# A one-layer streaming encoder step: adds that read PSUM become ScalarE copies and GpSimd adds, squares and norms of output rows stand half a block later, and two tiles' last products come before their norms

## The chip, the cores and the metric

One core of one Trainium2 chip runs the whole program. The metric is the device time of one execution in microseconds, median of several runs. The kernel before takes 1325.29 us (three runs, 1322.95 to 1325.57).

## What is computed

One layer with three branches over a prompt of 2048 tokens (batch 1) and a sample group of 64 tokens with a cache of 1024. Everything is float32. Cut to what matters here:

```
h = rms_norm(x, g_norm);  z = h @ w_in            # 1024 -> 3072
q_sb, k_sb, v_sb, g_sb, u_pool, g_pool, q_xa, g_xa = split(z)
# stick-breaking attention, 8 heads of 64, strictly causal:
s = q_sb . k_sb / 8
w = exp(log_sigmoid(s) + sum over later keys of log_sigmoid(-s))
o_sb = w @ v_sb
o_pool = pooling mixer(u_pool);  o_xa = softmax attention over 256 memory tokens
mixed = concat[o_sb * silu(g_sb), o_pool * silu(g_pool), o_xa * silu(g_xa)]
y = rms_norm(x + mixed @ w_out, g_final)          # the final norm, row by row
```

The outputs are y for both groups, the new key and value rows, the pooling history and the memory keys and values.

## The kernel before

Products are made of two or three float32r passes (a high and a low part of each factor), so TensorE has several matmuls per tile of the result. Up to about 690 us the kernel norms x, makes the projections of `w_in`, the pooling branch, the cross-attention and the sample group's attention. The change touches only what follows: the stick-breaking attention of the prompt, with the output product `mixed @ w_out` run beside it, and a tail that holds the last four row tiles' output product.

**The attention stage.** The prompt's queries go in four stages `s` of 512 tokens (0 to 3). A stage goes over four pairs of heads `p`, and for each over key blocks `j` of 512 from the diagonal back to 0. `Block.score` makes the scores of 128 queries by 512 keys for two heads in a PSUM tile `z` (two of them), `weigh` lets ScalarE take the sigmoid into a slot of the ring `c` (L207) and VectorE run the product from the last key to the first as two scans (L212 on the diagonal, L214 elsewhere). A half-block (`Stream.step`) is two such 128-query tiles, so four scans. Three half-blocks later (`TURN`) `turn` transposes the weights on TensorE into PSUM tiles `pt`, ScalarE copies them to `w` (L230), and `gather` multiplies them with differences of values into `av` (L241), one PSUM buffer. At the last key block of a pair, L252 on VectorE adds `vt` to `av`, which frees `av`; GpSimd multiplies with the gate (L258) and stores to `mix_d` (L259). In the trace's names `at_hl`, `at_hh`, `more_c` and `ends` are slots of these rings.

**The output rows.** From the second stage on, `Rows` holds one tile of 128 tokens of the stage before (12 such tiles, and one of 64 for the sample group). `split` makes its high and low parts: a ScalarE cast (L1098), a GpSimd subtraction (L1099). `piece` makes one of 16 products (two halves of 512 columns, eight each) into `acc`, one PSUM buffer (L1119). At the eighth, L1122 on VectorE adds `acc` to the row in `xt`, which frees `acc`, and L1123 squares the half with a sum. After the second half, `finish` makes the inverse root on VectorE (L1131 and L122 to L131), scales both halves (L1135) and has GpSimd's queue store the row (L1139).

**What sets the order.** For TensorE, ScalarE and VectorE the written order is the program's order in this part; GpSimd's and SyncE's instructions are placed by a scheduler. `Stream.step` writes a half-block: transposes, scores, scans, then as many pieces as `credit` allows (a `None` behind each half's last piece ends a run), then the products with values. The code written inside a piece lands on VectorE behind the scans of that half-block.

**The tail.** With `done` set, `z` takes the place of `acc`, so two tiles can be open at once. `most` makes the first seven products of both halves, `rest_of` the last ones, which need the last pair's result, and then the norm, with a square root on ScalarE (`root_of`).

Of the kernel before, what the change touches and what calls it, by code (L numbers as in the profile page):

```python
# [13 lines left out]
ALU = mybir.AluOpType  # L14
# [4 lines left out]
P = 128  # L19
# [5 lines left out]
KT = D // P  # L25
# [18 lines left out]
def tile_hybrid_step(  # L44
# [30 lines left out]
    V, A, G, PE = nc.vector, nc.scalar, nc.gpsimd, nc.tensor  # L75
# [100 lines left out]
    class Block:  # L176


        def __init__(self, a, j):
            self.a, self.j = a, j  # L180
            p, room = a["p"], a["room"]
            self.K = room("K").rearrange("p (a t) -> p a t", a=2)
            dma(f(self.K), k_d[p][:, j])
            self.V = f(room("V")).rearrange("p (b d) -> p b d", b=4)
            dma(self.V, dv_d[p][:, j])
            self.diag = j == a["s"]
            self.later, a["c"] = a["c"], [None] * 4
# [46 lines left out]
        def gather(self, kb, i0, turned):  # L234

            a, j = self.a, self.j
            room, p, s = a["room"], a["p"], a["s"]
            if self.diag and kb == 0:
                a["av"] = room("av")
            for h, rows in enumerate((LO, HI)):  # L240
                PE.matmul(  # L241
                    a["av"][rows, i0 * P :], self.V[:, kb, rows], turned[:, h, i0 * P :],
                    start=(self.diag and kb == 0), stop=(j == 0 and kb == 3),
                )
            if j == 0 and kb == 0:
                cols = slice(512 * s, 512 * s + 512)
                a["vt"], a["sg"] = room("vt"), room("sg")
                dma(a["vt"], vt_d[p][:, cols])
                dma(a["sg"], sg_d[p][:, cols])
            if j == 0 and kb == 3:  # L250
                o = room("o")
                V.tensor_tensor(o, a["av"], a["vt"], ALU.add)  # L252
                if (s, p) == LAST:

                    V.tensor_tensor(o, o, a["sg"], ALU.mult)
                    last_mixed.append(o)
                else:
                    G.tensor_tensor(o, o, a["sg"], ALU.mult)  # L258
                    store(mix_d[s][:, p], o)  # L259

    class Stream:
# [3 lines left out]


        def __init__(self, more):
            self.halves, self.pieces, self.credit = [], [], 0.0
            self.rate, self.more = 0.0, more

        def step(self, block, g):
            t = len(self.halves)
            self.halves.append((block, g))
            self.credit += self.rate
            turned = []
            b, old = self.halves[t - TURN] if t >= TURN else (None, 0)
            if b is not None:
                turned.append(b.turn(2 * old))
            if block is not None:
                first, second = block.score(2 * g), block.score(2 * g + 1)  # L280
                first()
            if b is not None:
                turned.append(b.turn(2 * old + 1))
            if block is not None:
                second()
                if g == 1:
                    block.cs = block.a["c"]
            self.run(self.credit)
            for what in turned:
                b.gather(*what)  # L290
            self.credit = min(self.credit, 6.0)

        def run(self, n):

            n = min(n, self.credit)
            while n >= 1.0 and self.piece():
                n -= 1.0
                self.credit -= 1.0

        def piece(self):  # L300

            if not self.pieces:
                self.pieces += self.more()
            if self.pieces:
                thunk = self.pieces.pop(0)
                if thunk is not None:
                    thunk()
                    return True
            return False
# [154 lines left out]
    def project(w, n, chunk):  # L464
        for piece in projection(w, n, chunk):
            acc = piece()
            slots.tick()
        return acc
# [180 lines left out]
    for c in range(2):  # L649
        for j in range(2):  # L650
            w, rows = WINDOWS[2 * c + j], slice(64 * j, 64 * j + 64)
# [115 lines left out]
    def cross(p, u, qx):  # L767
# [39 lines left out]
        for delay, stage, i in zip(XSLOTS, (scores, scores, turn, gather, turn, gather), (0, 1, 0, 0, 1, 1)):  # L807
            slots.after(delay, lambda stage=stage, i=i: stage(i))
# [214 lines left out]
    def room(name):  # L1023
        if name == "pt":
            return ps_t.tile([P, 512], F32, tag="pt", name="pt")
        rings[name].append(rings[name].pop(0))
        return rings[name][-1]


    wo = {}  # L1030

    def wo_part(c, part):
        return wo[(c // 4, part)][:, D * (c % 4) : D * (c % 4) + D]
# [14 lines left out]
    class Rows:  # L1048
# [56 lines left out]
        def piece(self, half, c):  # L1105
            n, xt = self.n, self.xt
            cols = slice(512 * half, 512 * half + 512)
            if c == 0 and done and half == 0:
                self.z = room("z")
            if c == 0 and not done:  # L1110
                self.acc = room("acc")
            k = self.ks[c]
            out, mh, ml = self.z[:, half] if done else self.acc, self.mh[:, k], self.ml[:, k]
            wh, wl = wo_part(k, "h")[:, cols], wo_part(k, "l")[:, cols]
            passes = [(out, mh, wh), (out, ml, wh)][: 2 if n == P else 1] + [(out[:n], mh[:, :n], wl)]
            if c == 7:
                passes.reverse()
            for i, (o, m, w) in enumerate(passes):
                PE.matmul(o, m, w, start=(c == i == 0), stop=(c == 7 and i == len(passes) - 1))  # L1119
            if c == 7:  # L1120
                for i in range(0, P, n):
                    V.tensor_tensor(xt[:n, cols], out[i : i + n], xt[:n, cols], ALU.add)  # L1122
                V.scalar_tensor_tensor(  # L1123
                    wo["sq"][:n, cols], xt[:n, cols], 1.0, xt[:n, cols], ALU.mult, ALU.mult,
                    accum_out=self.total[:n, half : half + 1],
                )

        def finish(self):
            n, xt = self.n, self.xt
# [14 lines left out]
    def follow():  # L1144
        if ready and not following:
            following.append(Rows(ready.pop(0)))

    def output_rows():

        if len(settled) >= SETTLED:  # L1150
            follow()
        if not following:
            return []

        if not done and len(stream.halves) - following[0].born < 2:
            return []
        rows = following.pop()
        while rows.parts:
            rows.split()
        pieces = []  # L1160
        for half in range(2):
            for c in range(KT):

                def piece(half=half, c=c):
                    rows.piece(half, c)
                    i = KT * half + c
                    if i == 1:
                        follow()
                    elif i > 3 and (i - 1) % 3 == 0 and following:
                        following[0].split()  # L1170
                    if i == 15:
                        rows.finish()

                pieces.append(piece)
                if c == KT - 1 and not done:
                    pieces.append(None)
        return pieces

    ready, done = [], False
# [17 lines left out]
    stream, tail = Stream(more), []  # L1197
# [19 lines left out]
    def prepared(t, *parts):  # L1217
        rows = Rows(t, parts)
        while rows.parts:
            rows.split()  # L1220
        tail.append(rows)
# [5 lines left out]
            tail[0].split()  # L1227
    while stream.pieces or ready or following:
        stream.piece()
    tail[0].split_late()  # L1230
    tail.append(Rows(T // P - 3, ("K", "K")))


    done = True

    def most(rows):
        for half in range(2):
            for c in range(KT - 1):
                rows.piece(half, c)

    def rest_of(rows):
        for half in range(2):
            rows.piece(half, KT - 1)
        rows.finish()

    for half in range(2):
        for c in range(KT - 1):
# [4 lines left out]
    prepared(T // P - 2, "K", "K")  # L1252
    tail[2].split_late()
    most(tail[1])
    rest_of(tail[0])
    rest_of(tail[1])
    prepared(T // P - 1, "q", "q")
    tail[3].split_late()
    for rows in tail[2:]:
        most(rows)  # L1260
        rest_of(rows)
# [32 lines left out]
```

## Time and profile before

| what | value |
|---|---|
| median of the runs | 1325.29 us |
| the profiled execution | 1323.47 us, of which 1321.7 us span from the first to the last instruction |
| mean granted TensorE clock | 0.981 |
| busy in the span | TensorE 1236.6 us (94%), VectorE 799.7 (61%), ScalarE 520.5 (39%), GpSimd 338.6 (26%) |
| VectorE's scans, L214 (192) and L212 (128) | 252.6 us and 103.8 us, all in the attention |

The span divides into the stages of the attention by the first sigmoid of each: stage 0 from 687 us, stage 1 from 753 us, stage 2 from 857 us, stage 3 from 1039 us, the tail from 1261 us. Busy shares over the whole span say little here, since VectorE is nearly unused in some stretches and nearly full in others: the stage in which an instruction stands has to be looked at by itself. A wait of TensorE is shown with the instruction that ended it, which can be queued behind others on its own engine.

### The profile page before, as it was taken

The page shows a single profiled execution, that of the slowest core. Times are in us where ns is not written, and L with a number is a line of the kernel's source. Part 1 is how long each engine was busy: PE and PEld are TensorE (multiplying, and loading weights), DVE is VectorE, ACT ScalarE, POOL GpSimd, SP SyncE. Part 2 cuts the span into 40 slices and gives each one's busy share as a digit, 9 for nine tenths or more (in the row PEclk, how much of TensorE's full clock was granted, in tenths as well). Part 3 has the DMA queues.
Part 4 walks back from the last instruction along what each step waited for, and adds up shares of the span by engine and source line. Part 5 has one row for each costly group of instructions (what it writes and reads, how often), then busy time and mean ns, then how long its engine had stood idle before and what let it go on. Part 6 is the DMA issues. An engine that isn't in the chain of part 4 may idle for free.

```text
span 1321.7 us, 22014 instructions
## 1 busy us (share of the span) xinstructions
PE 1236.6 (94%) x8506; PEld 954.7 (72%) x8506; DVE 799.7 (61%) x1388; ACT 520.5 (39%) x1077; POOL 338.6 (26%) x415
## 2 busy tenths in 40 slices
PE   5899999999999999999999988999988998999987
PEld 5788888688888888887887755666655655666565
DVE  7863445455554442333224596779987787899644
ACT  5641111144444442231013464446445465576510
POOL 3211237234444442222001113321312002012110
PEclk9999999999999999999999999989999998999999
DMA  7534432555555543443256774434443243431221
GB/s 243 189 121 151 150 132 82 172 177 194 172 167 160 171 143 125 146 131 107 87 182 212 286 269 135 154 104 147 134 136 116 101 127 120 136 112 51 93 74 49
DMA packets 115637, 190.30 MB, mean 144 GB/s; under 512 B 9458, under 2 KB 73548, under 8 KB 115532
## 3 DMA queue, kind: packets, MB, share of 16 engines
q1 hardware_dynamic: 95436, 120.95, 29.9%
q0 software_dynamic: 20096, 67.94, 14.2%
q8 instruction: 67, 1.10, 0.4%
q14 instruction: 38, 0.31, 0.1%
HBM read 118.83 MB, written 70.02 MB: 143 GB/s over the span
## 4 chain that ended last, share of the span: by engine, by line
PE 59%; DVE 10%; issue 7%; ACT 4%; POOL 3%; DMA 3%; DVEq 0%; ACTq 0%; SPq 0%; POOLq 0%
PE acc L1119 11%; PE acc L441 8%; PE acc L443 7%; PE acc L442 7%; PE av L241 7%; DVE at_hl L214 5%; PE pt L227 5%; PE z L198 4%; PE z L1119 3%; ACT more_w L230 2%; ACT at_hl L207 1%; POOL psum_w L669 1%; PE pt_p L787 1%; PE pt_r L477 1%; DVE xo L1122 1%
## 5 line engine op out<-in xcount | busy, mean ns | idle before, releaser
L441 PE MATMUL acc<-hh,wh 128*128 128x512 f32 (+2 forms) x960 | 358.3, 374 | 6.5 <-DVE sg L543 5.5
L442 PE MATMUL acc<-hl,wh 128*128 128x512 f32 (+2 forms) x960 | 341.9, 356 | 0.0
L443 PE MATMUL acc<-hh,wl 128*128 128x512 f32 (+2 forms) x960 | 339.9, 355 | 0.0
L230 ACT COPY more_w<-pt 128x512 f32<-128x512 f32 (+3 forms) x320 | 152.0, 528 | 216.6 <-PE pt L227 214.7
L214 DVE TENSOR_TENSOR_SCAN at_hl<-at_hl,at_hl 128x512 f32<-128x512 f32 x148 | 195.1, 1375 | 25.3 <-ACT at_hl L207 25.3
L441 PEld LDWEIGHTS acc<-hh,wh 128*128 128x128 f32 x960 | 182.0, 190 | 32.4 <-DVE sg L543 8.1
L443 PEld LDWEIGHTS acc<-hh,wl 128*128 128x128 f32 x960 | 181.7, 189 | 24.5 <-issue 1.0
L442 PEld LDWEIGHTS acc<-hl,wh 128*128 128x128 f32 x960 | 182.5, 190 | 21.1 <-issue 4.0
L241 PE MATMUL av<-more_w,at_hh 128*64 128x512 f32 (+3 forms) x640 | 140.0, 551 | 11.3 <-DVE ends L252 8.6
L227 PEld LDWEIGHTS pt<-edge,at_hl 64*128 64x128 f32 x1936 | 87.9, 139 | 60.6 <-issue 44.8
L207 ACT ACTIVATE at_hl<-z 128x1024 f32<-128x1024 f32 (+3 forms) x143 | 130.8, 916 | 0.6
L212 DVE TENSOR_TENSOR_SCAN at_hl<-at_hl,edge 128x128 f32<-128x128 f32 (+3 forms) x116 | 92.8, 852 | 34.4 <-ACT at_hl L207 34.4
L1119 PE MATMUL acc<-at_hh,mh 128*128 128x512 f32 x208 | 92.0, 442 | 19.2 <-DVE xo L1122 14.4
L227 PE MATMUL pt<-edge,at_hl 64*128 64x64 f32 x1936 | 102.3, 228 | 5.5 <-ACT more_w L230 3.7
L1099 POOL TENSOR_TENSOR ml<-m,mh 128x256 fp32r<-128x256 f32 (+1 forms) x52 | 58.9, 1144 | 169.2 <-ACT mh L1098 169.0
L241 PEld LDWEIGHTS av<-more_w,at_hh 128*64 128x64 f32 x640 | 37.9, 137 | 79.3 <-issue 48.1
L1119 PE MATMUL acc<-at_hl,mh 128*128 128x512 f32 (+1 forms) x208 | 84.3, 418 | 0.0
L1119 PE MATMUL acc<-at_hh,ml 128*128 128x512 f32 x192 | 79.5, 414 | 1.0 <-POOL ml L1099 1.0
L198 PE MATMUL z<-at_hh 64*128 64x512 f32 (+2 forms) x576 | 70.2, 375 | 0.0
L432 DVE CAST wh<-wr 128x1024 fp32r<-128x1024 f32 x32 | 23.6, 736 | 70.5 <-PE acc L442 34.2
L1119 PEld LDWEIGHTS acc<-at_hh,mh 128*128 128x128 f32 x208 | 41.8, 201 | 32.5 <-DVE xo L1122 15.7
L543 DVE TENSOR_TENSOR sg<-acc,sg 128x512 f32<-128x512 f32 x24 | 16.5, 690 | 69.9 <-ACT sg L542 69.9
(275 smaller groups left out, 1808.0 us busy)
## 6 DMA issues: line engine op xcount, KB each, us to landing
at_hh<-k_d SPq DMA_DIRECT2D x40, 512.0 KB, 5.3
wr<-in_w_in_dram SPq DMA_DIRECT2D x24, 512.0 KB, 4.7
at_hh<-dv_d SPq DMA_DIRECT2D x40, 256.0 KB, 3.5
xt_x<-in_x_prompt_dram SPq DMA_DIRECT2D x16, 512.0 KB, 4.0
xq<-qx_d SPq DMA_DIRECT2D x64, 128.0 KB, 4.0
k_d<-k POOLq DMA_DIRECT2D x16, 512.0 KB, 3.8
out_dram<-rt POOLq DMA_DIRECT2D x32, 256.0 KB, 3.5
q_d<-q POOLq DMA_DIRECT2D x16, 512.0 KB, 2.9
```

Source lines behind the costliest of these rows:

```text
L198: PE.matmul(z[:, h, :w], a["q"][rows, part, at], K[rows, keys, :w], start=(part == keys == 0), stop=(part == 1),)
L207: A.activation(c[:, :, :n], z[:, :, :n], AF.Sigmoid, scale=-1.0)
L212: V.tensor_tensor_scan(cc, cc, edge[:, 512 - n :][:, ::-1], 0.0, ALU.mult, ALU.max)
L214: V.tensor_tensor_scan(cc, cc, cc, self.later[i][:, h, 0:1], ALU.mult, ALU.bypass)
L227: PE.transpose(pt[:, h, i], c, ident[rows, rows])
L230: A.copy(w[:, :, i0:, rows], pt[:, :, i0:])
L241: PE.matmul(a["av"][rows, i0 * P :], self.V[:, kb, rows], turned[:, h, i0 * P :], start=(self.diag and kb == 0), stop=(j == 0 and kb == 3),)
L441: PE.matmul(out, wh[:, k], hi, start=(k == 0), stop=False)
L442: PE.matmul(out, wh[:, k], lo, start=False, stop=False)
L443: PE.matmul(out, wl[:, k], hi, start=False, stop=(k == KT - 1))
L1099: engine.tensor_tensor(ml, m, f(mh), ALU.subtract)
L1119: PE.matmul(o, m, w, start=(c == i == 0), stop=(c == 7 and i == len(passes) - 1))
```

## The change

Four edits:

- In `gather`, L252's add on VectorE becomes a ScalarE copy of `av` into `o` and a GpSimd add of `vt` (15 of 16; the last pair of the last stage keeps the old form).
- In `Rows.piece`, for the 12 tiles of 128 rows beside the attention (24 halves), L1122's add becomes a ScalarE copy of `acc` into `wo["sq"]` and a GpSimd add into `xt`. The sample tile and the tail keep the old form.
- For those 24 halves the square, and for all 13 tiles the norm (`finish`), go to a list `due`, which is written out by `settle` in the next half-block, behind that half-block's scans.
- In the tail, `rest_of` takes the first two tiles together: both tiles' last products, adds and squares are written before both norms.

```diff
@@ gather
             if j == 0 and kb == 3:
                 o = room("o")
-                V.tensor_tensor(o, a["av"], a["vt"], ALU.add)
                 if (s, p) == LAST:
 
+                    V.tensor_tensor(o, a["av"], a["vt"], ALU.add)
                     V.tensor_tensor(o, o, a["sg"], ALU.mult)
                     last_mixed.append(o)
                 else:
+                    A.copy(o, a["av"])
+                    G.tensor_tensor(o, o, a["vt"], ALU.add)
                     G.tensor_tensor(o, o, a["sg"], ALU.mult)
                     store(mix_d[s][:, p], o)
@@ Stream.step
                 second()
                 if g == 1:
                     block.cs = block.a["c"]
+            self.settle()
             self.run(self.credit)
...
+        def settle(self):
+
+            while self.due:
+                self.due.pop(0)()
@@ Rows.piece
             if c == 7:
-                for i in range(0, P, n):
-                    V.tensor_tensor(xt[:n, cols], out[i : i + n], xt[:n, cols], ALU.add)
-                V.scalar_tensor_tensor(
-                    wo["sq"][:n, cols], xt[:n, cols], 1.0, xt[:n, cols], ALU.mult, ALU.mult,
-                    accum_out=self.total[:n, half : half + 1],
-                )
+                if n == P and not done:
+
+                    A.copy(wo["sq"][:, cols], out)
+                    G.tensor_tensor(xt[:, cols], wo["sq"][:, cols], xt[:, cols], ALU.add)
+                    stream.due.append(lambda: self.square(half))
+                else:
+                    for i in range(0, P, n):
+                        V.tensor_tensor(xt[:n, cols], out[i : i + n], xt[:n, cols], ALU.add)
+                    self.square(half)
+
+        def square(self, half):
+            n, cols = self.n, slice(512 * half, 512 * half + 512)
+            V.scalar_tensor_tensor(
+                wo["sq"][:n, cols], self.xt[:n, cols], 1.0, self.xt[:n, cols], ALU.mult, ALU.mult,
+                accum_out=self.total[:n, half : half + 1],
+            )
@@ output_rows
                     if i == 15:
-                        rows.finish()
+                        stream.due.append(rows.finish)
@@ the tail
-    def rest_of(rows):
-        for half in range(2):
-            rows.piece(half, KT - 1)
-        rows.finish()
+    def rest_of(*tiles):
+        for rows in tiles:
+            for half in range(2):
+                rows.piece(half, KT - 1)
+        for rows in tiles:
+            rows.finish()
...
-    rest_of(tail[0])
-    rest_of(tail[1])
+    rest_of(*tail[:2])
```

The order of TensorE's instructions is the same in both programs. Three places on the other engines show the move. In the changed file the lines are L258 to L260 (copy, add and product of the attention result), L1131 and L1132 (copy and add of a row half), L1136 (the add that stays), L1141 (square), L1149 and L1153 (norm). The order view names the scans SCALAR_TENSOR_TENSOR.

VectorE, end of the second row tile (stage 1), before: the last steps of its norm, then the attention add, the four scans of the next half-block, and the add and square of the third tile's first half.

```order
L130 TENSOR_TENSOR nr_t<-nr_t,nr_y 128x1
L131 SCALAR_TENSOR_TENSOR nr_y<-nr_t,nr_y 128x1
L1135 SCALAR_TENSOR_TENSOR xo<-xo,nr_y,gf 128x512 x2
L252 TENSOR_TENSOR at_hl_6504<-av,ends 128x512
L214 SCALAR_TENSOR_TENSOR at_hl_6504<-at_hl_6504,at_hl_6506 128x512 x4
L1122 TENSOR_TENSOR xo<-acc_6518,xo 128x512
L1123 SCALAR_TENSOR_TENSOR sq,total_o<-xo 128x512
```

The norm stood ahead of the half-block's scans, and the two adds that free `av` and `acc` stood between and behind scans. VectorE, the same tile, now:

```order
L212 SCALAR_TENSOR_TENSOR at_hl_6506<-at_hl_6506,edge 128x512 x2
L1141 SCALAR_TENSOR_TENSOR sq,total_o<-xo 128x512
L214 SCALAR_TENSOR_TENSOR more_c_6512<-more_c_6512,at_hl_6506 128x512 x2
L214 SCALAR_TENSOR_TENSOR at_hl_6504<-at_hl_6504,at_hl_6506 128x512 x6
L1141 SCALAR_TENSOR_TENSOR sq,total_o<-xo 128x512
L1149 TENSOR_TENSOR total_s<-total_o 128x1
```

No add is left among the scans; the second square and the norm follow the scans of one more half-block. ScalarE, same place, now, where the two copies (L1131 of `acc`, L258 of `av`) stand between one half-block's second sigmoid and the next one's copies of transposes:

```order
L207 ACTIVATE more_c_6512<-z_6515 128x1024
L230 COPY more_w<-pt 128x8x64 x2
L207 ACTIVATE at_hl_6504<-z_6516 128x1024
L1131 COPY sq<-acc_6518 128x512
L258 COPY at_hl_6504<-av 128x512
L230 COPY more_w<-pt 128x8x64 x2
```

Before, nothing stood there. VectorE in the tail, now, from the first tile's second half to the first norm:

```order
L1136 TENSOR_TENSOR xo<-z_6515,xo 128x512
L1141 SCALAR_TENSOR_TENSOR sq,total_o<-xo 128x512
L1136 TENSOR_TENSOR at_hl_6506<-z_6516,at_hl_6506 128x512
L1141 SCALAR_TENSOR_TENSOR sq,total_o<-at_hl_6506 128x512
L1149 TENSOR_TENSOR total_s<-total_o 128x1
L139 TENSOR_SCALAR nr_v<-total_s 128x1
```

Before, the first tile's whole norm stood ahead of the second tile's first add.

## Rows read from the trace of the kernel before

**Rows 1.** Waits of TensorE, 753 to 1321 us: total us, times, longest.

```profile
PE acc L1119 <- DVE xo L1122: 14.4, 9, 3.5
PE av L241 <- DVE ends L252: 8.6, 3, 4.1
```

**Rows 2.** The same by stretch: 857 to 1039, 753 to 793, 1039 to 1245.

```profile
PE acc L1119 <- DVE xo L1122: 11.0, 5, 3.5
PE av L241 <- DVE ends L252: 4.1, 1, 4.1
...
PE av L241 <- DVE ends L252: 2.7, 1, 2.7
PE av L241 <- DVE at_hl L252: 0.9, 1, 0.9
...
PE acc L1119 <- DVE xo L1122: 2.9, 3, 1.8
```

**Rows 3.** Busy us by stretch: PE, PEld, DVE, ACT, POOL, then clock, DMA, GB/s.

```profile
753.00:793.00 40.00, 35.12 (x392) 22.02 (x392) 36.38 (x39) 28.06 (x56) 7.34 (x6) 0.96 0.83 291
793.00:857.00 64.00, 58.38 (x448) 40.41 (x446) 45.26 (x72) 28.54 (x56) 20.00 (x18) 0.97 0.44 143
857.00:1039.00 182.00, 166.17 (x1397) 110.10 (x1393) 151.02 (x215) 90.42 (x168) 42.70 (x38) 0.95 0.41 126
1039.00:1245.00 206.00, 196.25 (x1793) 124.53 (x1792) 177.23 (x234) 122.47 (x211) 29.60 (x29) 0.98 0.36 110
```

**Rows 4.** Timeline of VectorE and TensorE around 857 us: start, us, what.

```profile
854.01 6.62 DVE L214 TENSOR_TENSOR_SCAN at_hl<-at_hl,at_hl 128x512 f32<-128x512 f32 x4
860.56 0.66 DVE L1122 TENSOR_TENSOR xo<-acc,xo 128x512 f32<-128x512 f32 x1
...
861.27 0.80 PE L1119 MATMUL acc<-at_hh,mh 128*128 128x512 f32 x1 [3.47 <-DVE xo L1122]
```

**Rows 5.** Busy us in stretches of half clock (columns as in Rows 3).

```profile
860.70:867.40 6.70, 6.13 (x14) 4.79 (x15) 3.03 (x7) 0.00 (x0) 0.45 (x1) 0.50 0.13 51
925.60:928.90 3.30, 3.30 (x10) 2.11 (x9) 3.30 (x3) 0.00 (x0) 2.25 (x2) 0.50 0.36 97
973.30:976.70 3.40, 3.40 (x16) 1.00 (x18) 3.40 (x3) 0.00 (x0) 2.65 (x3) 0.50 0.65 239
1024.50:1027.90 3.40, 3.25 (x8) 2.57 (x9) 3.37 (x6) 0.00 (x0) 0.04 (x1) 0.50 0.07 29
1065.50:1068.80 3.30, 3.30 (x10) 2.17 (x10) 3.30 (x5) 0.00 (x0) 0.00 (x0) 0.50 0.45 133
...
1287.40:1290.70 3.30, 3.30 (x8) 2.62 (x9) 2.19 (x7) 0.01 (x1) 0.00 (x0) 0.50 0.27 103
```

**Rows 6.** Groups by shape, 753 to 1250: count | busy us, mean ns | idle before.

```profile
L214 DVE TENSOR_TENSOR_SCAN at_hl<-at_hl,at_hl 128x512 f32<-128x512 f32 x148 | 195.1, 1375 | 25.3 <-ACT at_hl L207 25.3
...
L1122 DVE TENSOR_TENSOR xo<-acc,xo 128x512 f32<-128x512 f32 x23 | 15.4, 667 | 18.3 <-PE acc L1119 18.3
...
L252 DVE TENSOR_TENSOR at_hl<-av,ends 128x512 f32<-128x512 f32 x7 | 4.7, 675 | 0.3 <-issue 0.3
...
L230 ACT COPY more_w<-pt 128x512 f32<-128x512 f32 x214 | 115.1, 590 | 169.2 <-PE pt L227 168.3
```

**Rows 7.** Timeline: VectorE's scans and GpSimd's products, 757 to 771 us.

```profile
767.46 1.27 DVE L214 TENSOR_TENSOR_SCAN at_hl<-at_hl,at_hl 128x512 f32<-128x512 f32 x1
768.65 2.22 DVE L214 TENSOR_TENSOR_SCAN at_hl<-at_hl,at_hl 128x512 f32<-128x512 f32 x1
...
757.09 1.27 POOL L258 TENSOR_TENSOR at_hl<-at_hl,ends 128x512 f32<-128x512 f32 x1 [4.11 <-DVE at_hl L252]
...
767.63 2.16 POOL L258 TENSOR_TENSOR ends<-ends 128x512 f32<-128x512 f32 x1 [8.39 <-DVE ends L252]
```

**Rows 8.** Timeline of VectorE and TensorE in the tail.

```profile
1283.97 0.16 DVE L1131 TENSOR_TENSOR total_s<-total_o 128x1 f32<-128x1 f32 x1
...
1286.60 0.68 DVE L1122 TENSOR_TENSOR at_hl<-z,at_hl 128x512 f32<-128x512 f32 x1
...
1287.34 0.80 PE L1119 MATMUL z<-at_hl,at_hh 128*128 128x512 f32 x1 [4.18 <-DVE at_hl L1122]
```

More of the change, by code (lines that the diff above doesn't have):

```diff
@@ L267, in __init__ @@
         def __init__(self, more):
-            self.halves, self.pieces, self.credit = [], [], 0.0
+            self.halves, self.pieces, self.credit, self.due = [], [], 0.0, []
             self.rate, self.more = 0.0, more
@@ L1229, in tile_hybrid_step @@
         stream.piece()
+    stream.settle()
     tail[0].split_late()
```

## The prediction

> **What bounds the kernel now.** I read the waits of TensorE first, because TensorE is busy almost throughout the part that the change touches. From 753 us on it loses 14.4 us in nine waits for L1122, the add that frees `acc`, and 8.6 us in three for L252, the add that frees `av` [rows 1]; a fourth wait for L252, of 0.9 us, stands in the early stretch [rows 2]. That is 23.9 us. The timeline shows what such a wait is. At 857.8 us TensorE wants `acc`. The add takes only 0.66 us, but it stands behind four scans that began at 854.01 and took 6.62 us [rows 4]. So the wait is VectorE's queue, not the add.
>
> Next I read the granted clock behind these waits. After five of them TensorE runs at half clock, 1.2 instead of 2.4 GHz, for 6.7, 3.3, 3.4, 3.4 and 3.3 us [rows 5]. TensorE is at work nearly all of those 20.1 us, so the level costs half of them, about 10.0 us.
>
> Last, the busy time by stretch. From 753 to 793 us VectorE is busy 36.38 of 40 us, 91%: there it is the bound, and a wait of TensorE only says where TensorE meets it. From 857 to 1039 us it has 151.02 of 182 us, from 1039 to 1245 us 177.23 of 206, from 793 to 857 us 45.26 of 64 [rows 3].
>
> **The copies on ScalarE.** 39 copies of 128x512 from PSUM are added; copies of this shape take 0.590 us in the mean [rows 6]. Each stands behind the half-block's second sigmoid and ahead of copies for which ScalarE waits on TensorE anyway (168.3 us of such waits [rows 6]). I cost them at nothing. If that cover were gone they would cost 39 x 0.59 = 23 us. What they bring is that `acc` and `av` come free about 0.8 us after their last product, while TensorE has other products and transposes to do. I take both kinds of wait as gone, with the low clock behind them, except where VectorE binds.
>
> **The adds on GpSimd and VectorE's load.** VectorE sheds an add of 0.667 us (row halves) or 0.675 us (attention) [rows 6], 39 in all: 14 from 857 to 1039 us, 12 from 1039 to 1245, 6 from 793 to 857, 3 from 753 to 793, the others at the two ends. GpSimd takes an add of the size of its product L258: 1.27 us when no scan runs beside it, 2.16 us beside scans. The scan beside the latter takes 2.22 us, where the one before it took 1.27 [rows 7]: 0.95 us lost on VectorE. No row shows what an added add will cost VectorE. It lies between 0 (GpSimd meets no scan) and 0.95 (it always does). I take 0.95, since scans are most of VectorE's work there. The trade is then 0.95 - 0.67 = 0.28 us more of VectorE's time per add, not less.
>
> The Trainium skill (SBUF — State Buffer, Who interferes with whom) says that a VectorE instruction with two SBUF inputs and a GpSimd instruction that reads SBUF exclude each other for a whole instruction. By that rule a scan could lose the add's full 1.27 us. The trace agrees in kind, with 0.95 us measured; by the full price the gain of the stretch from 857 us would be about 6.6 us in place of the 11.6 worked out next.
>
> **The sum by stretch.** *857 to 1039 us.* Without its waits (11.0 + 4.1 [rows 2]) and half of its 16.8 us at low clock [rows 5], TensorE would need 182 - 15.1 - 8.4 = 158.5 us. VectorE would need 151.0 + 14 x 0.28 = 154.9 us, which is 98% of that. It was never nearly so full: where it bound, it reached 91%. I take that share: 154.9 / 0.91 = 170.4 us (with the share unrounded), a gain of 11.6 us. The other 12 come back as waits of transposes for scans (L227 on L214), and I expect some low clock to stay with them. *1039 to 1245 us.* The waits are 2.9 us [rows 2], the clock 3.3 / 2 = 1.7. VectorE would need (177.2 + 12 x 0.28) / 0.91 = 198.6 us, less than TensorE's 201.4: a gain of 4.6 us. *793 to 857 us.* Left of the totals are 14.4 - 11.0 - 2.9 = 0.5 us for `acc` and 8.6 - 4.1 - 2.7 = 1.8 us for `av`; VectorE has room: 2.3 us. *753 to 793 us.* VectorE binds already; nothing of the 2.7 + 0.9 us is gained, and 3 x 0.28 / 0.91 = 0.9 us is lost.
>
> **Squares and norms later.** These are the same instructions on VectorE, so they cost no busy time; they let the next scans go first, which is part of what lets TensorE run ahead. Behind each later norm is the row's store in GpSimd's queue, and behind that the next adds and splits. Four scans took 6.62 us [rows 4], so a store may come that much later. A split is used a row later; I cost the delay at nothing, and at 6.6 us apiece where it isn't so (a rival).
>
> **The tail.** At 1287.34 us TensorE has waited 4.18 us for the second tile's first add. That add began at 1286.60 us, behind the first tile's norm, which began at 1283.97 [rows 8]. Without the norm in front it begins 2.63 us earlier: 2.6 us. The wait left is 1.55 us. Whether the 3.3 us of low clock behind it [rows 5] goes too I leave to the range (1.7 us).
>
> Sum: 11.6 + 4.6 + 2.3 - 0.9 + 2.6 = 20.2 us. The profiled execution took 1323.47 us, of which 1321.7 is its span, and would take 1303.3. It lies 1.8 us under the median of the runs, 1325.29, so for the median I predict **1305 us**.
>
> **Rivals.** *VectorE isn't the bound.* The half-blocks' slack takes up its lag, GpSimd meets few scans, and every wait and clock loss goes: 15.1 + 8.4 + 4.6 + 2.3 + 3.6 + 2.6 + 1.7 = 38.3 us, so 1287 us. For it: in VectorE's 31 us of idle time from 857 to 1039 us are waits for the very products (18.3 us over all stretches, L1122 on `acc` [rows 6]) that the change takes off it. Against it: 98% would be a load without any hole.
>
> *GpSimd's queue.* The later norm holds the row's store, and the first splits of a stage's first row stand behind it. Three such places at 6.62 us [rows 4] would eat 19.9 us and leave 1325 us. Against it: the norm of the row before is mostly long done when a stage begins.
>
> *Slower: VectorE's idle time is structural.* VectorE waits 25.3 us for sigmoids of a fresh half-block ahead of the scans of L214 alone [rows 6]. If those holes stay, VectorE is the bound already and keeps its present shares. Each add's 0.28 us then lengthens the stretches: 154.9 / 0.830 = 186.7 (+4.7), 180.6 / 0.860 = 209.9 (+3.9), 46.9 / 0.707 = 66.4 (+2.4), +0.9 early, less the tail's 2.6: 9.3 us slower, 1335 us. It decides as soon as TensorE, freed from the adds, waits for scans instead of running ahead. For it is 753 to 793 us, where that is so; against it, that the longer waits from 857 us on end with an add, not with a scan [rows 2, 4]. The Trainium skill (Perfetto Trace Analysis, Optimizing Scalar/DVE Operations) warns of this trade: VectorE and GpSimd share a read port, so that moving operations between the two might not help. The trace bears that out for the scan that took 2.22 us.
>
> **Chances and range.** The forecast has 0.56; its own range, with VectorE's share between 0.87 and 0.95 from 857 to 1039 us (gains of 4 to 19 us there), is 1297 to 1313. VectorE not the bound has 0.22, GpSimd's queue 0.10, slower 0.12. A difference of 0.2% (2.7 us) is about what a measurement of this kernel can tell from no change. The forecast and the first rival are faster; the second is mostly within (0.08 of its 0.10, the rest on either side); the third is slower. That makes 0.79 faster, 0.08 within, 0.13 slower. The range reaches down to the first rival and up to the second's edge, 1287 to 1324; it leaves out the slower rival and some of the second.
>
> **What would show it.** The waits of `acc` on L1122 and of `av` on L252 should be gone from TensorE's list, ScalarE's copies taking their place with under 2 us in all. Scans should be longer in the mean than 1375 ns, GpSimd's adds about 2 us each. From 857 to the start of the fourth stage VectorE should be about 91% busy, and waits of transposes for scans should be the longest left. In the tail the wait of 4.18 us should be near 1.6. The prediction is wrong if the stretch from 857 us takes 160 us (VectorE had the room), or 180 and more (it had none), or if TensorE comes to wait for L1107's splits on GpSimd.

## The result and the profile after

The changed kernel takes 1305.20 us (four runs, 1303.61 to 1307.54) where the kernel before, run beside it, takes 1324.12: a ratio of 0.986 (95% interval 0.9841 to 0.9879), 18.6 us faster. The profiled execution took 1306.19 us with a span of 1304.5. The forecast was 1305. That it came out so closely is partly luck: the sum took 20.2 us off the span, the profile has 17.2 us, and the terms were off in both directions. So the profile has to be read by stretch.

In the changed file TensorE's product of row tiles is L1127, its splits are L1106 and L1107, ScalarE's copy of `acc` is L1131, GpSimd's add L1132, the add that kept the old form L1136, the square L1141. First the waits of TensorE, 754 to 1304.5 us (total us, times, longest), the answer to [rows 1]:

```profile
PE pt L227 <- DVE at_hl L214: 7.7, 8, 2.1
PE acc L1127 <- DVE xo L1136: 7.2, 2, 5.1
PE acc L1127 <- ACT mh L1106: 4.8, 2, 2.4
...
PE z L1127 <- DVE at_hl L1136: 2.2, 2, 1.4
PE acc L1127 <- POOL ml L1107: 1.7, 2, 1.0
PE av L241 <- ACT more_w L230: 1.6, 8, 0.2
```

No wait of `av` for an add is left. Of the nine waits of `acc` seven are gone. The two that stayed are for L1136, the add in its old form: they belong to the 64-row sample tile, and one of them is now the longest wait of all, 5.1 us. Waits of transposes for scans (L227 on L214) have become the largest sum. Most of that lies in the early stretch. From 754 to 796 us, and then from 859 to 1032 us:

```profile
PE pt L227 <- DVE at_hl L214: 5.5, 5, 2.1
...
PE pt L227 <- DVE at_hl L214: 2.2, 3, 0.9
```

Busy us by stretch, with the bounds at the same half-blocks as in [rows 3] (us, PE, PEld, DVE, ACT, POOL, clock, DMA, GB/s):

```profile
754.28:796.24 41.96, 35.79 (x384) 22.23 (x382) 37.26 (x36) 29.21 (x58) 12.24 (x9) 0.95 0.83 290
796.24:859.24 63.00, 59.51 (x455) 41.46 (x453) 44.01 (x50) 32.44 (x65) 29.86 (x26) 0.95 0.40 125
859.24:1032.18 172.94, 162.73 (x1393) 107.66 (x1389) 151.30 (x214) 97.50 (x181) 62.90 (x50) 0.97 0.43 136
1032.18:1220.03 187.85, 182.64 (x1705) 116.78 (x1707) 170.78 (x201) 123.37 (x215) 49.79 (x40) 0.98 0.35 110
```

The fourth ends at the last half-block; the same one of before, for which [rows 3] has another end:

```profile
1039.08:1232.88 193.80, 185.04 (x1705) 117.77 (x1707) 167.13 (x226) 117.25 (x203) 29.04 (x28) 0.97 0.35 108
```

With before's bounds at the same half-blocks (753.45, 793.20, 857.29, 1039.08, 1232.88) the stretches changed by +2.2, -1.1, -8.9 and -6.0 us, and what follows, to the end of the span, from 88.8 to 84.5: -4.3.

The groups by shape, 753 to 1250 us (count, busy us, mean ns, idle before), answer to [rows 6]:

```profile
L214 DVE TENSOR_TENSOR_SCAN at_hl<-at_hl,at_hl 128x512 f32<-128x512 f32 x148 | 206.8, 1456 | 35.1 <-ACT at_hl L207 34.8
...
L1132 POOL TENSOR_TENSOR xo<-sq,xo 128x512 f32<-128x512 f32 x24 | 39.2, 1635 | 81.5 <-ACT sq L1131 81.3
...
L1131 ACT COPY sq<-acc 128x512 f32<-128x512 f32 x24 | 14.4, 598 | 19.6 <-PE acc L1127 19.6
```

A scan is 81 ns longer in the mean than before, an add on GpSimd takes 1.64 us in the mean.

The timeline at the longest wait (start, us, what):

```profile
917.34 1.42 DVE L1153 SCALAR_TENSOR_TENSOR xo<-xo,nr_y,gf 128x512 f32<-128x512 f32 x2
918.67 7.19 DVE L214 TENSOR_TENSOR_SCAN at_hl<-at_hl,at_hl 128x512 f32<-128x512 f32 x4
925.78 1.38 DVE L1136 TENSOR_TENSOR xo<-acc,xo 64x512 f32<-64x512 f32 x2
...
920.45 2.18 POOL L259 TENSOR_TENSOR at_hl<-at_hl,ends 128x512 f32<-128x512 f32 x1
922.71 2.07 POOL L260 TENSOR_TENSOR at_hl<-at_hl,ends 128x512 f32<-128x512 f32 x1
...
927.22 0.80 PE L1127 MATMUL acc<-at_hh,mh 128*128 128x512 f32 x1 [5.09 <-DVE xo L1136]
```

It is the picture of [rows 4] again, with more in front: the sample tile's two adds stand behind four scans, the scans behind a norm that was moved there, and the scans take 7.19 us, since two GpSimd operations on an attention result run beside them (without these, in an experiment below, they take 5.24 us). Stretches in which TensorE works at half clock (columns as above):

```profile
795.20:798.60 3.40, 3.09 (x28) 2.52 (x26) 2.95 (x5) 2.01 (x4) 0.00 (x0) 0.50 0.71 271
802.00:805.40 3.40, 3.19 (x8) 2.52 (x9) 1.23 (x1) 0.00 (x0) 3.13 (x4) 0.50 0.00 0
890.80:894.20 3.40, 3.38 (x26) 2.68 (x28) 3.40 (x3) 2.10 (x3) 0.00 (x0) 0.50 0.73 185
924.90:931.70 6.80, 4.48 (x11) 3.03 (x12) 6.73 (x9) 0.00 (x0) 2.01 (x3) 0.50 0.95 293
```

The last, of 6.8 us, goes with the sample tile's wait; before, 3.3 us at 925.6 us [rows 5] followed the same tile's wait of 1.84 us. The first and the third stand behind short waits for scans (1.03 and 0.71 us; 0.76 and 0.87 us), the second behind waits for the splits of a stage's first tile (2.43 and 0.99 us), as before. Two more, at 774.7 and 1092.1 us, have their like before. Those behind the removed waits at 860, 973, 1024 and 1065 us [rows 5] are gone.

The tail, which answers to [rows 8]:

```profile
1271.29 0.68 DVE L1136 TENSOR_TENSOR at_hl<-z,at_hl 128x512 f32<-128x512 f32 x1
...
1274.37 0.15 DVE L1149 TENSOR_TENSOR total_s<-total_o 128x1 f32<-128x1 f32 x1
...
1272.03 0.50 PE L1127 MATMUL z<-at_hl,at_hh 128*128 128x512 f32 x1 [1.42 <-DVE at_hl L1136]
```

The second tile's first add no longer waits for the first tile's norm, which now starts 3.1 us after it: the wait fell from 4.18 to 1.42 us, and the half clock behind it is gone.

### The profile page after: what moved, and what is told of

Same layout as the page of the kernel before. It is cut to its first block, busy times and chain, and to the rows that moved or that the text cites. A ratio compares the mean times of both kernels' runs of the same rounds, so it can differ in the third digit from the quotient of the medians.

```text
span 1304.5 us, 22169 instructions
## 1 busy us (share of the span) xinstructions
PE 1231.0 (94%) x8506; PEld 951.4 (73%) x8506; DVE 804.6 (62%) x1349; ACT 541.2 (41%) x1116; POOL 399.2 (31%) x454
## 5 line engine op out<-in xcount | busy, mean ns | idle before, releaser
L214 DVE TENSOR_TENSOR_SCAN at_hl<-at_hl,at_hl 128x512 f32<-128x512 f32 x148 | 206.8, 1456 | 35.1 <-ACT at_hl L207 34.8
L227 PEld LDWEIGHTS pt<-edge,at_hl 64*128 64x128 f32 x1936 | 88.8, 140 | 66.6 <-issue 44.0
L212 DVE TENSOR_TENSOR_SCAN at_hl<-at_hl,edge 128x128 f32<-128x128 f32 (+3 forms) x116 | 101.6, 932 | 24.0 <-ACT at_hl L207 24.0
L227 PE MATMUL pt<-edge,at_hl 64*128 64x64 f32 x1936 | 104.1, 230 | 11.4 <-DVE at_hl L214 7.7
L1127 PE MATMUL acc<-at_hh,mh 128*128 128x512 f32 x208 | 89.4, 430 | 12.0 <-DVE xo L1136 7.2
L1107 POOL TENSOR_TENSOR ml<-m,mh 128x256 fp32r<-128x256 f32 (+1 forms) x52 | 60.1, 1165 | 108.8 <-ACT mh L1106 108.6
L1127 PE MATMUL acc<-at_hl,mh 128*128 128x512 f32 (+1 forms) x208 | 82.5, 410 | 0.0
L1127 PE MATMUL acc<-at_hh,ml 128*128 128x512 f32 x192 | 77.3, 403 | 1.7 <-POOL ml L1107 1.7
L1132 POOL TENSOR_TENSOR xo<-sq,xo 128x512 f32<-128x512 f32 x24 | 39.2, 1635 | 81.5 <-ACT sq L1131 81.3
L1127 PEld LDWEIGHTS acc<-at_hh,mh 128*128 128x128 f32 x208 | 40.8, 196 | 24.7 <-DVE xo L1136 7.5
```

What stands on the lines that cost most here:

```text
L212: V.tensor_tensor_scan(cc, cc, edge[:, 512 - n :][:, ::-1], 0.0, ALU.mult, ALU.max)
L214: V.tensor_tensor_scan(cc, cc, cc, self.later[i][:, h, 0:1], ALU.mult, ALU.bypass)
L227: PE.transpose(pt[:, h, i], c, ident[rows, rows])
L1107: engine.tensor_tensor(ml, m, f(mh), ALU.subtract)
```

## The experiments

All ratios are to the kernel before, run on the same chip. Three chips were used, so kernels are compared by ratio, and by time only where they ran beside each other. The changed kernel once more is the scale.

> The changed kernel again, as the scale for the three beside it: a ratio of 0.986 to the kernel before by either theory.

Measured: 0.9853 (0.9837 to 0.9869).

**One part alone: the tail.** The kernel before with the new `rest_of`.

> The kernel before with one part alone: in the tail the last products and adds of both of the first two tiles ahead of their norms. Theory A: TensorE's wait of 4.18 us falls to 1.4 to 1.6 us, and with it goes the 3.3 us at half clock behind it: 2.6 to 4.3 us faster, a ratio of 0.9967 to 0.998. Theory B (the last tiles wait for their splits or weights anyway, so that the end stays): within 1 us.

Measured: 0.9969 (0.9957 to 0.9981), some 4 us. The wait is 1.43 us, and no half clock follows it. Theory A, at its upper end.

**One part alone: the attention results.** The kernel before with only this:

```diff
-                V.tensor_tensor(o, a["av"], a["vt"], ALU.add)
+                    A.copy(o, a["av"])
+                    G.tensor_tensor(o, o, a["vt"], ALU.add)
```

> The kernel before with one part alone: the attention results copied by ScalarE and added on GpSimd (15 of them); row halves and tail as before. Theory A (waits that go are gained where VectorE isn't the bound): of TensorE's four waits for `av`, 3.6 us early aren't gained, 4.1 + 1.8 us are, with 3.3 us of clock behind the one at 860 us: 5 to 9 us faster, 1315 to 1319. Theory B (each wait removed comes back as a wait for a scan): within 2 us of before.

Measured: 1.0019 (1.0004 to 1.0034): not faster, rather 2.5 us slower. Theory B, a little beyond its 2 us. The waits of TensorE, 753 to 1322 us:

```profile
PE acc L1127 <- DVE xo L1130: 19.4, 9, 3.5
PE pt L227 <- DVE at_hl L214: 6.4, 7, 2.1
```

L1130 is the old add of row halves here. All 8.6 us of `av` are gone, but `acc` waits 19.4 us where it waited 14.4 [rows 1], and 6.4 us of waits for scans stand beside them. At 969 us before, TensorE waited 4.08 us for `av`, and 23 us later 0.73 us for `acc`; now it doesn't wait at the first place, and 2.89 us at the second. Here VectorE's lag behaves as one quantity, which TensorE pays at the next thing that it needs from VectorE.

**One part alone: squares and norms later,** all adds still on VectorE.

> The kernel before with one part alone: squares and norms half a block later, all adds still on VectorE where they were. Theory A (the adds themselves must leave VectorE's queue: TensorE waits for an add behind four scans, and the square and the norm come after it): within 3 us of before, 1321 to 1327. Theory B (the norm ahead of the scans is what made VectorE late): 5 to 10 us faster, 1314 to 1319.

Measured: 0.9995 (0.9981 to 1.0008), nothing. Theory A. The same exchange the other way, in its waits:

```profile
PE acc L1124 <- DVE xo L1127: 13.5, 8, 3.4
PE acc L1124 <- DVE xo L1131: 6.1, 2, 3.2
...
PE av L241 <- DVE ends L252: 2.8, 1, 2.8
```

The waits for `av` outside the early stretch go (0.45 us is left of them), and those for `acc` grow to 13.5 + 6.1 us, the second for the sample tile.

**One part alone: row halves** by ScalarE and GpSimd, the square in its old place.

```diff
-                    V.tensor_tensor(xt[:, cols], out, xt[:, cols], ALU.add)
+                    A.copy(wo["sq"][:, cols], out)
+                    G.tensor_tensor(xt[:, cols], wo["sq"][:, cols], xt[:, cols], ALU.add)
                     self.square(half)
```

> The kernel before with one part alone: a row half is copied out of `acc` by ScalarE and added on GpSimd, but its square and the norm stay where they were, so VectorE's next instruction in its queue waits for GpSimd's add. Theory A (the later squares are what the gain hangs on, since in place VectorE stands still for the copy and the add, some 0.6 + 1.3 to 2.1 us for each of 24 halves, ahead of scans that TensorE wants): 0 to 25 us slower than before, 1324 to 1350. Theory B (the early release of `acc` alone brings the gain, and VectorE has the room): 8 to 14 us faster, 1310 to 1316.

Measured: 0.9939 (0.9921 to 0.9957), some 8 us faster: theory B by the time, at the lower end of its 8 to 14 us. What theory A names is there too. VectorE does stand still at the squares (L1138) for GpSimd's adds (L1129), 33.9 us from 753 to 1250:

```profile
L1138 DVE SCALAR_TENSOR_TENSOR sq<-xo 128x512 f32<-128x512 f32 x23 | 20.7, 900 | 33.9 <-POOL xo L1129 33.9
```

TensorE feels it where the add that frees `av` is queued behind the square and the norm. Its waits, and VectorE's timeline at one of 2.99 us that begins at 821.05:

```profile
PE av L241 <- DVE ends L252: 10.4, 4, 4.4
```

```profile
818.73 0.69 DVE L1138 SCALAR_TENSOR_TENSOR sq<-xo 128x512 f32<-128x512 f32 x1 [1.81 <-POOL xo L1129]
...
821.98 1.41 DVE L1150 SCALAR_TENSOR_TENSOR xo<-xo,nr_y,gf 128x512 f32<-128x512 f32 x2
823.31 0.68 DVE L252 TENSOR_TENSOR ends<-av,ends 128x512 f32<-128x512 f32 x1
```

**Without the attention results.** The changed kernel with L252's add back on VectorE. So it is rows, later squares and tail.

> The changed kernel without one part: the attention results are added by VectorE straight from `av` in its queue, as before; row halves and tail as changed. By itself that part gained nothing (1.0019). Theory A (TensorE pays VectorE's lag at whichever add it meets first, so the part is worth something only once `acc` is free of adds): the waits for `av` come back, 8 to 11 us in all, and the kernel is 5 to 10 us slower than the changed one, a ratio of 0.989 to 0.993. Theory B (the part is worth nothing in either company): within 2 us of the changed kernel, 0.984 to 0.987.

Measured: 0.9803 (0.9786 to 0.9819), 1298.37 us: by the ratios faster than the changed kernel (0.986 and 0.9853) by 0.5%, with intervals that don't meet. Both theories fall. This part of the change costs some 6.5 us. First TensorE's waits of the whole (753 to 1325), then the timeline of VectorE at the sample tile:

```profile
PE acc L1124 <- DVE xo L1133: 5.1, 2, 3.2
...
PE av L241 <- DVE ends L252: 2.8, 1, 2.8
...
PE pt L227 <- DVE at_hl L214: 2.3, 2, 1.5
```

```profile
912.38 5.24 DVE L214 TENSOR_TENSOR_SCAN at_hl<-at_hl,at_hl 128x512 f32<-128x512 f32 x4
917.54 1.38 DVE L1133 TENSOR_TENSOR xo<-acc,xo 64x512 f32<-64x512 f32 x2
```

L1133 is the add in the old form here. Of `av` only the early waits (2.76 and 0.88 us) are back, and 0.43 us later: where squares and norms come later, L252 is early enough in VectorE's queue. The four scans ahead of the sample tile's adds take 5.24 us, not 7.19, and the wait behind them 3.16, not 5.09. By stretch, the changed kernel's four against this one's 39.94, 61.82, 169.78 and 188.15 us: +2.0, +1.2, +3.2, -0.3.

Against the kernel with row halves alone (67.31, 173.76 and 191.47 us from the second stretch on), the later squares took 5.5, 4.0 and 3.3 us off; the tail's edit lies behind these. That is 12.8 us from single profiles; the ratios, 0.9939 - 0.9803 less the tail's 0.0031, give some 14 us. So the later squares, worth nothing alone, are worth 13 to 14 us once `acc` is free of adds and the attention results are still added by VectorE.

**Without the later squares.** The changed kernel with `self.square(half)` and `rows.finish()` in place.

> The changed kernel without one part: squares and norms stand in VectorE's queue where they were before, right behind the product, so that each square waits there for ScalarE's copy and GpSimd's add. Rows alone with squares in place made VectorE wait 38.1 us in eight places (10.2 us in two in the changed kernel). Theory A (that standing time delays scans that TensorE wants): 4 to 10 us slower than the changed kernel, 0.988 to 0.993. Theory B (it falls into VectorE's idle time): within 2 us, 0.984 to 0.987.

Measured: 0.9851 (0.9833 to 0.9868), the changed kernel's time. Theory B by the time; by stretch two things cancel. At the sample tile the norm stands four scans earlier in VectorE's queue and the first wait is 2.84 us, not 5.09; that stretch takes 169.9 us, 3 less; the stretch behind it takes 189.8 in place of 187.9. Later squares and result copies remove the same waits for `av`. Added to the row halves, the result copies without the later squares are worth 0.9939 - 0.9851 less the tail's 0.0031, some 7.5 us (an estimate, since rows and tail alone were not run); together with the later squares they cost some 6.5 us. With the copies in place the later squares bring nothing.

**The sample tile.** What the forecast left over in 859 to 1032 us was put to the test from here on. The changed kernel, and for the 64 rows:

```diff
+                elif not done:
+                    for i in range(2):
+                        part = wo["sq"][:n, 512 * (half ^ i) : 512 * (half ^ i) + 512]
+                        A.copy(part, out[n * i : n * i + n])
+                        G.tensor_tensor(xt[:n, cols], part, xt[:n, cols], ALU.add)
+                    stream.due.append(lambda: self.square(half))
```

> The changed kernel, with the 64-row sample tile's four adds moved off VectorE too: each half is read out of `acc` by two ScalarE copies, added by two GpSimd adds of 64x512, and squared half a block later. Theory A (VectorE's load bounds 859 to 1032 us): VectorE sheds 4 x 0.69 us and loses about as much in scans beside the four added adds, so 0 to 1 us faster, about 1304. Theory B (what the stretch still loses is the sample tile's two waits of TensorE, 5.09 + 2.09 us, and half of the 6.8 us at half clock behind the first): both waits go from TensorE's list, 7 to 11 us faster, 1295 to 1298.

Measured: 0.9822 (0.9808 to 0.9837), 3.9 us under the changed kernel beside it. Theory B by what goes (both waits, and half of the 6.8 us at half clock), but by less than its 7 to 11 us. Waits of TensorE in 859 to 1028 us, and the scans:

```profile
PE pt L227 <- DVE at_hl L214: 4.8, 5, 1.7
```

```profile
927.35 3.90 DVE L214 TENSOR_TENSOR_SCAN at_hl<-at_hl,more_c 128x512 f32<-128x512 f32 x2
931.17 3.82 DVE L214 TENSOR_TENSOR_SCAN at_hl<-at_hl,at_hl 128x512 f32<-128x512 f32 x2
```

The scans take 1.9 us each: the first two beside the product of an attention result and splits, which GpSimd's new adds push back by 3.4 us, the last two beside a new add. 2.6 us of waits for scans at 932 and 933 us take the place of part of the sample tile's 7.2.

**The same, with the four adds on VectorE,** half a block later.

> The changed kernel, with the sample tile's accumulators read by ScalarE copies, and its four adds left on VectorE but half a block later, ahead of their squares. With the four adds on GpSimd the sample tile's waits went but only 3.9 us of the 7 to 11 did. Theory A (there GpSimd's four adds of some 3 us each stretched the scans, and scans became the wait): without them 6 to 9 us faster than the changed kernel, 1295 to 1298. Theory B (VectorE's queue is the bound there, whoever adds): 3 to 5 us faster, 1299 to 1301, with the same waits of transposes for scans at 932 to 935 us.

Measured: 0.9819 (0.9799 to 0.9839), 1297.46 us. By the ratios it can't be told from the one above, so the time doesn't decide. The profile speaks for theory A: the waits for scans at 932 us are gone (one of 1.45 us for a ScalarE copy is left), and the stretch takes 166.0 us against 168.7 with GpSimd's adds.

```profile
857.58:1023.59 166.01, 161.13 (x1393) 106.45 (x1389) 154.43 (x214) 99.56 (x185) 64.43 (x50) 0.99 0.44 142
```

VectorE is busy 154.43 of 166.01 us here, 93%.

**All row adds on VectorE,** the sample tile's too, from ScalarE's copies.

> The changed kernel, with all row halves, the sample tile's too, copied out of `acc` by ScalarE and added by VectorE half a block later, none on GpSimd (only the attention results are). Moving the 24 row adds off GpSimd alone changed nothing (ratio 0.9859 against 0.9853); the sample tile by itself gave 0.982. Theory A (a GpSimd add costs VectorE in scans what VectorE's own add would, so that who adds is all one): within 2 us of the kernel with only the sample tile's adds so, a ratio of 0.981 to 0.983. Theory B (GpSimd's adds cost more where VectorE is full, which the sample tile's waits hid): 3 to 6 us faster still, 0.977 to 0.980.

Measured: 0.9814 (0.9797 to 0.9831). Theory A: with the sample tile's waits out of the way, too, the time is the same whoever adds the row halves.

**The price of an add on GpSimd.** The changed kernel, with the 24 adds on VectorE half a block later:

```diff
-                    G.tensor_tensor(xt[:, cols], wo["sq"][:, cols], xt[:, cols], ALU.add)
+                    stream.due.append(lambda: V.tensor_tensor(xt[:, cols], wo["sq"][:, cols], xt[:, cols], ALU.add))
                     stream.due.append(lambda: self.square(half))
```

> The changed kernel, with the 24 adds of row halves not on GpSimd: ScalarE's copy out of `acc` stays, and VectorE adds the copy half a block later, ahead of the square. It prices the GpSimd adds. If each costs VectorE 0.95 us in stretched scans against the 0.67 us it saves (the prediction's price) and VectorE bounds (theory A), 24 x 0.28 us go: 4 to 7 us faster, 1298 to 1301. If VectorE isn't the bound but for single places (theory B): within 2 us of the changed kernel. If the 0.95 us is too high a price (adds stand mostly beside nothing): VectorE's 16 us more of adds make it 5 us slower or more.

Measured: 0.9859 (0.9844 to 0.9874) beside 0.9853: no difference, theory B by the time. But VectorE's load did move. The two long stretches, in the changed kernel's second profile and then here:

```profile
858.69:1031.61 172.92, 162.71 (x1393) 107.79 (x1389) 151.34 (x214) 97.49 (x180) 63.14 (x50) 0.97 0.43 136
1031.61:1218.12 186.51, 181.27 (x1707) 115.62 (x1708) 171.56 (x201) 123.18 (x216) 51.45 (x40) 0.99 0.36 111
```

```profile
857.03:1029.71 172.68, 162.16 (x1393) 107.41 (x1389) 148.00 (x223) 97.51 (x180) 44.14 (x40) 0.97 0.42 133
1029.71:1216.74 187.03, 181.93 (x1705) 115.97 (x1707) 169.10 (x209) 123.17 (x215) 36.38 (x32) 0.99 0.36 111
```

GpSimd has 10 + 8 instructions fewer, and VectorE is 3.34 + 2.46 = 5.80 us less busy although it does those adds now: 5.80 / 18 = 0.32 us per add in VectorE's favour. The scans say where from:

```profile
L214 DVE TENSOR_TENSOR_SCAN at_hl<-at_hl,at_hl 128x512 f32<-128x512 f32 x148 | 193.3, 1366 | 38.0 <-ACT at_hl L207 38.0
```

A scan is back at 1366 ns from 1456.

**Twice the adds on GpSimd.**

```diff
                     G.tensor_tensor(xt[:, cols], wo["sq"][:, cols], xt[:, cols], ALU.add)
+                    G.tensor_tensor(wo["sq"][:, cols], wo["sq"][:, cols], xt[:, cols], ALU.add)
```

> The changed kernel, with one more GpSimd add of 128x512 behind each of the 24 adds of row halves (its sum goes to scratch and is not used; the outputs are computed as before). Theory A: each costs VectorE 0.95 us of scans, 22.8 us in all, and with VectorE at its bound 10 to 20 us of them are seen: 1315 to 1325. Theory B: VectorE has 13% of idle time from 859 to 1032 us, which takes them: 0 to 5 us slower, up to 1310.

Measured: 0.9932 (0.9919 to 0.9946), 1314.29 us: 10.0 us slower than the changed kernel, between the theories, next to A. TensorE's waits for scans from 754 to 1312 us, then the two long stretches:

```profile
PE pt L227 <- DVE at_hl L214: 13.8, 13, 3.2
...
855.90:1034.62 178.72, 164.11 (x1393) 108.46 (x1389) 159.23 (x214) 97.50 (x181) 81.53 (x60) 0.96 0.43 135
1034.62:1226.03 191.41, 183.32 (x1705) 116.32 (x1707) 180.06 (x201) 123.17 (x215) 71.83 (x49) 0.99 0.34 107
```

In these two stretches 19 more adds made VectorE 7.89 + 8.50 = 16.4 us busier, 0.86 us each, and the stretches 5.8 + 4.9 = 10.7 us longer. It is not GpSimd's own queue: TensorE's waits for its splits (L1107) stayed at 1.6 us, against 1.8, while those for scans grew from 7.7 to 13.8 us. So less load on VectorE gave nothing, and of more load two thirds were seen: that is how an engine at the edge of being the bound, and not beyond it, would look.

## Why the prediction was right, and where it was not

**Right: what the waits were.** It read the waits for `acc` and `av` as VectorE's queue and not as the adds. The parts run alone show it more strictly than it was put: taking one kind of wait away moves the lag to the other.

**Right: the trade of 0.28 us per add.** It set 0.95 us of scan lost beside a GpSimd add against 0.67 us shed. Measured were 0.86 us per added add and, with the adds taken back, 0.32 us net. The 0.95 came from one scan, and GpSimd's adds took 1.64 us in the mean where about 2 were expected; so the close fit is partly luck. ScalarE's copies took 0.598 us where 0.590 was set, and cost nothing that a wait shows.

**Wrong: "I take both kinds of wait as gone".** Two of the nine waits for `acc` are the sample tile's, whose adds the change leaves on VectorE; the text on the change says so, and the sum overlooked it. Their 1.84 + 1.95 us are in the 15.1 us that the sum takes off TensorE from 857 us on, with the half clock behind the first. They grew to 5.09 + 2.09 us. In front of them the change put a norm and GpSimd work that stretches the scans.

**Wrong: "I take that share", 91% of VectorE as the bound from 857 us.** The stretch came to 172.9 us, near the 170.4 forecast, but at 87.5%: the size came out near by luck, from another cause. Of its 14.4 us over TensorE's 158.5, the sample tile's waits and half of the 6.8 us at half clock are 10.6. The scans that were named have 2.2 us of waits and half of 3.4 us at half clock behind two of them. With the sample tile's adds out of the way VectorE reached 93%, and the stretch took 166.0 us. Without its waits of 2.7 + 2.2 us and half of 3.4 us at half clock that is 159.4, so the 158.5 for TensorE alone was good.

**Wrong: gains counted for the attention results.** The sum took `av`'s waits of 4.1 + 1.8 us behind the early stretch as theirs, though it let part of the first come back as waits for scans. The later squares alone leave 0.45 us of these. So in the changed kernel the result copies gain nothing: they cost 2.0 us early, where VectorE binds (0.9 was set, the sign was right), 1.2 us from 793 to 857 and 3.2 us in the stretch of the sample tile. "They cost no busy time" was right of the later squares and said too little: with the row halves they bring 13 to 14 us where the result copies are left out.

**The other terms.** 1039 us to the last half-block: 4.6 set (to 1245 us), 6.0 measured, with VectorE at 91% and TensorE at 97%. 793 to 857: 2.3 set, 1.1 measured; two stretches at half clock fall between 795 and 805 us where before had one. Tail: 2.6 set, 4.3 measured, since the half clock behind the wait, left to the range, went too. So the total of 20.2 against 17.2 us of span came from terms off by 1.2 to 2.7 us in both directions.

**The rivals.** "GpSimd's queue" falls: for the splits of a stage's first tile TensorE waits 2.4 us for ScalarE's cast in two stages, as before, and for GpSimd's part (L1107) 1.0 and 0.8 us, where before it was 1.0 us in one stage: 0.8 us more in all. "Slower" holds for the early stretch only, and for the attention results alone. "VectorE isn't the bound" was half right: it isn't beyond its limit, and the time is held by single places, but the gain stayed at half of the 38.3 us.

**Left open.** Row halves and later squares without the result copies, together with the sample tile's adds moved, was not tried. The kernel without result copies has the lowest ratio (0.9803) and beats the changed kernel; from the kernels with the sample tile's adds moved (0.9814 to 0.9822) it can't be told apart.

## What to carry to other kernels

A wait that stands behind a queue is the queue's lag, paid at the first thing that is needed from it: price the removal of all such things together, since one alone may return nothing and the last may be worth most. When an edit covers "most" of the instances of a line, look for the ones that it leaves, and for what it puts in front of them. Of two edits that remove the same wait keep the one that costs the loaded engine nothing: here the later order, not the copy of the attention results with its adds on GpSimd.

## What the runs showed of the hardware

That GpSimd and VectorE slow each other isn't one-sided. In the kernel with the sample tile's adds on GpSimd, an add of 64x512, which took 1.28 us at its shortest, took 9.75 us beside scans that ran at full speed:

```profile
936.33 9.75 POOL L1138 TENSOR_TENSOR xo<-sq,xo 64x512 f32<-64x512 f32 x1 [2.43 <-ACT sq L1137]
...
935.50 7.15 DVE L214 TENSOR_TENSOR_SCAN at_hl<-at_hl,at_hl 128x512 f32<-128x512 f32 x6
```

Six scans in 7.15 us are 1.19 us from one to the next, where in the changed kernel two of the four at 918.67 took 2.2 us each beside the operations on a result. (Spans on GpSimd are rough; that VectorE's square waited until 946.12 us for this add bears this one out.) So in these runs an add on GpSimd cost a scan up to a microsecond (2.2 us in place of 1.27), or nothing at all and then itself came late. What decides which, no run here shows.
